# Small SBUF-to-SBUF copies on ScalarE's DMA queue while the first tiles are loaded

## The chip, the cores and the metric

One core of a Trainium2 chip runs the kernel. The metric is the device time of one execution in microseconds (us). Most of the work here is done by the core's 16 DMA engines, which move data between HBM and the on-chip SBUF; VectorE (DVE) and ScalarE (ACT) calculate, and SyncE (SP) and ScalarE issue the transfers. A transfer that is issued is cut into packets, each engine works through its share of them, and a semaphore tells when all have landed.

## The reference

Each of the 32 x 512 = 16384 rows of 1024 float32 values is divided by the sum of its absolute values:

```python
sums = np.sum(np.abs(x), axis=-1, keepdims=True)
return (x / (sums + 1e-8)).astype(np.float32)
```

The input is 67.11 MB and so is the output. Every byte goes through SBUF once.

## The kernel before

The 16384 rows are cut into 11 tiles (`rows`, line 31): ten of 12 rows per partition (128 x 12 x 1024, 6.29 MB) and a last one of 8 (4.19 MB). Four buffers of 48 KB per partition hold the tiles in turn (line 42). A tile goes through three steps.

- `load` (line 84) issues one transfer on SP's queue. `max_dma_last_dim` sets the longest piece that one packet moves: 49152 bytes for tiles 0 and 1, 24576 for the others.
- `compute` (line 97) calls `normalize` (line 45). VectorE sums the absolute values (line 47), adds the small constant (line 54), takes the reciprocal (line 56) and multiplies most rows of the tile in place (lines 58 and 65). In tiles 0 to 2 and the last two ScalarE multiplies a few rows itself (line 68); `split` on line 76 says how many.
- `store` (line 88) issues the way back on ScalarE's queue, as one transfer, or as two halves of 6 rows for the fourth and the third tile from the end (`last - 3` and `last - 2`, tiles 7 and 8). All in all there are 13 stores and 11 loads.

The order is written out by hand (lines 102 to 109): loads 0 to 3, and then for each tile its calculation, its store and the load of the tile four further on, which takes the same buffer. So load 4 waits on SP's queue until store 0 is done, load 5 until store 1, and so on; the last four stores have no load behind them.

Each DMA engine serves SP's queue (q1 in the profile) and ScalarE's queue (q10). Within a queue the packets go in the order of issue. Each of the 24 transfers ends in a packet of 4 bytes on each engine that raises its semaphore (24 x 16 = 384 packets). There are eight such semaphores for transfers, dealt out in turn; a transfer whose semaphore was used before also waits for the transfer that used it.

Of the kernel before, what the change touches and what calls it, by code (L numbers as in the profile page):

```python
# [1 line left out]

# [4 lines left out]

FP32 = mybir.dt.float32
EPS = 1e-8


@with_exitstack
def kernel(
    ctx: ExitStack,
    tc: tile.TileContext,
    x: bass.AP,
    out: bass.AP,
):
    nc = tc.nc
    P = nc.NUM_PARTITIONS  # L20

    x_flat = x.flatten_outer_dims()
    out_flat = out.flatten_outer_dims()
    n, d = x_flat.shape

    R = 12
    BUFS = 4
    HEAD = 32
    per_partition = n // P
    assert n % P == 0 and (per_partition - HEAD) % R == 0  # L30
    rows = [R] * ((per_partition - HEAD) // R + 2) + [HEAD - 2 * R]

    def piece(flat, i):
        head = flat[: P * HEAD, :].rearrange("(p r) d -> p r d", p=P)
        if i < 2:
            return head[:, R * i : R * (i + 1), :]
        if i == len(rows) - 1:
            return head[:, 2 * R :, :]
        a = P * (HEAD + R * (i - 2))
        return flat[a : a + P * R, :].rearrange("(p r) d -> p r d", p=P)  # L40

    sbuf = ctx.enter_context(tc.tile_pool(name="sbuf", bufs=BUFS))
    stats = ctx.enter_context(tc.tile_pool(name="stats", bufs=len(rows)))

    def normalize(x_tile, k, kv, kt):
        s = stats.tile([P, R], FP32)
        nc.vector.tensor_reduce(  # L47
            out=s[:, :k],
            in_=x_tile[:, :k, :],
            axis=mybir.AxisListType.X,  # L50
            op=mybir.AluOpType.add,
            apply_absolute_value=True,
        )
        nc.vector.tensor_scalar_add(out=s[:, :k], in0=s[:, :k], scalar1=EPS)  # L54
        inv = stats.tile([P, R], FP32)
        nc.vector.reciprocal(out=inv[:, :k], in_=s[:, :k])  # L56
        if kv:
            nc.vector.tensor_mul(  # L58
                out=x_tile[:, :kv, :],
                in0=x_tile[:, :kv, :],  # L60
                in1=inv[:, :kv].unsqueeze(2).to_broadcast([P, kv, d]),
            )
        for r in range(kv, kv + kt):
            row = x_tile[:, r, :]
            nc.vector.tensor_scalar_mul(out=row, in0=row, scalar1=inv[:, r : r + 1])  # L65
        for r in range(kv + kt, k):
            row = x_tile[:, r, :]
            nc.scalar.activation(  # L68
                out=row,
                in_=row,  # L70
                func=mybir.ActivationFunctionType.Copy,
                scale=inv[:, r : r + 1],
            )

    last = len(rows) - 1
    split = {0: (3, 4), 1: (0, 3), 2: (0, 3), last - 1: (0, 2), last: (5, 3)}

    tiles = {}

    HALF, WHOLE = 24576, 49152

    def load(i):
        x_tile = tiles[i] = sbuf.tile([P, R, d], FP32, name="x_tile")
        nc.sync.dma_start(out=x_tile[:, : rows[i], :], in_=piece(x_flat, i), max_dma_last_dim=WHOLE if i < 2 else HALF)  # L86

    def store(i):
        parts = [(0, R // 2), (R // 2, R)] if i in (last - 3, last - 2) else [(0, rows[i])]
        for a, b in parts:  # L90
            nc.scalar.dma_start(
                out=piece(out_flat, i)[:, a:b, :],
                in_=tiles[i][:, a:b, :],
                max_dma_last_dim=WHOLE if i >= last - 1 else HALF,
            )

    def compute(i):
        k = rows[i]
        kt, ks = split.get(i, (0, 0))
        normalize(tiles[i], k, k - kt - ks, kt)  # L100

    with tc.manual_schedule():
        for i in range(BUFS):
            load(i)
        for i in range(len(rows)):
            compute(i)
            store(i)
            if i + BUFS < len(rows):
                load(i + BUFS)


# [1 line left out]
_INS = ['x']  # L113
_OUTS = [((32, 512, 1024), 'float32')]


# [23 lines left out]
```

## Time and profile before

| what | value |
|---|---|
| median of 3 runs | 317.03 us (316.71 to 317.07) |
| profiled execution | 316.79 us, of which span 315.2 us |
| VectorE busy | 261.1 us, 51 instructions |
| ScalarE busy | 17.4 us, 16 instructions |
| VectorE waits for loads | 30.0 us in total, 17.7 of it for tile 0 |
| HBM read and written | 67.11 and 67.11 MB, 426 GB/s over the span |
| a load, issue to landing | 37.6 us (median of ten) |
| a store, issue to landing | 47.2 us (median of eight whole tiles) |

The profile is that of one execution; all instants are counted from the start of its span. Issue to landing includes the time in which a transfer stands behind others in its queue, so it is longer than the 14.5 us that 6.29 MB take at 433 GB/s. In a table by windows the columns are: the window and its length, the busy time of VectorE, ScalarE and GpSimd with their instructions, a TensorE clock (which is not used here), the share of the 16 DMA engines' time that packets took, and the GB/s of the packets that started in the window. In the list of queues the columns are packets, MB and the share of the 16 engines' time. A timeline row is start, duration, engine, line and operation; `SPq` and `ACTq` are the issues of transfers by SP and ScalarE.

### The profile page before, as it was taken

Reading aid. Unit: us, or ns where it says so; the run is one execution under the profiler, and the core shown is the slowest. Engines: PE = TensorE matmul, PEld = TensorE weight load, DVE = VectorE, ACT = ScalarE, POOL = GpSimd, SP = SyncE. Lnnn points to the kernel's source line nnn. Section 1 sums busy time; section 2 is a strip of 40 time slices with the busy share of each in tenths; the row PEclk is TensorE's granted clock in tenths of the full one; section 3 lists DMA queues with packets and bytes.
Section 4 is the critical chain, followed back from the end, with each engine's and each line's share of the span. In section 5 each row is a group of like instructions: output and inputs, shape, how many; then the busy total and the mean of one; then the engine's idle time right before and its main releaser. Section 6 shows DMA issues by size and latency. Waiting matters only on the chain.

```text
span 315.2 us, 169 instructions
## 1 busy us (share of the span) xinstructions
DVE 261.1 (83%) x51; ACT 17.4 (6%) x16; POOL 0.2 (0%) x4
## 2 busy tenths in 40 slices
DVE  0079999999999999979996997999699969999100
ACT  0010403004000000000000000000000000203000
POOL 0000000000000000000000000000000000000000
DMA  7999999999999999999999999999999999999997
GB/s 299 499 399 409 440 399 418 430 449 418 430 449 418 430 449 424 424 449 427 421 449 427 421 449 434 415 449 434 415 449 434 415 433 449 416 433 499 399 403 329
DMA packets 5504, 134.22 MB, mean 426 GB/s; under 512 B 384, under 2 KB 384, under 8 KB 384
## 3 DMA queue, kind: packets, MB, share of 16 engines
q1 hardware_dynamic: 2736, 67.11, 49.9%
q10 hardware_dynamic: 2768, 67.11, 49.4%
HBM read 67.11 MB, written 67.11 MB: 426 GB/s over the span
## 4 chain that ended last, share of the span: by engine, by line
DVE 41%; DMA 33%; another core or an unknown queue 18%; SPq 0%; issue 0%; DVEq 0%
DVE s L47 23%; DMA x_tile<-in_x_dram 17%; DVE x_tile L58 15%; DMA out_dram<-x_tile 15%; DVE x_tile L65 2%; DVE inv L56 0%; DVE s L54 0%; SPq L86 0%; DVEq L135 0%
## 5 line engine op out<-in xcount | busy, mean ns | idle before, releaser
L47 DVE TENSOR_REDUCE s<-x_tile 128x12 f32<-128x12288 f32 (+1 forms) x11 | 138.2, 12561 | 30.0 <-DMA x_tile<-in_x_dram 30.0
L58 DVE TENSOR_TENSOR x_tile<-x_tile,inv 128x12288 f32<-128x12288 f32 (+3 forms) x10 | 113.6, 11358 | 0.5
L68 ACT ACTIVATE x_tile<-x_tile,inv 128x1024 f32<-128x1024 f32 x15 | 16.1, 1138 | 257.1 <-DVE inv L56 257.1
L65 DVE TENSOR_SCALAR x_tile<-x_tile,inv 128x1024 f32<-128x1024 f32 x8 | 5.5, 748 | 0.0
L56 DVE RECIPROCAL inv<-s 128x12 f32<-128x12 f32 (+1 forms) x11 | 2.5, 226 | 0.4
L68 ACT ACT_TABLE_LOAD x1 | 1.3, 1283 | 17.8 <-DMA x_tile<-in_x_dram 17.8
L54 DVE TENSOR_SCALAR s<-s 128x12 f32<-128x12 f32 (+1 forms) x11 | 1.9, 173 | 0.4
L124 POOL MEMSET const-uint8-127<- 128x1 uint8 x1 | 0.1, 102 | 0.0
L124 POOL MEMSET const-bfloat16-1.0<- 128x1 bf16 x1 | 0.1, 101 | 0.0
L124 POOL MEMSET const-float32-0.0<- 128x1 f32 x1 | 0.1, 98 | 0.2 <-issue 0.2
L124 POOL MEMSET const-float32-1.0<- 128x1 f32 x1 | 0.1, 98 | 0.0
## 6 DMA issues: line engine op xcount, KB each, us to landing
x_tile<-in_x_dram SPq DMA_DIRECT2D x10, 6144.0 KB, 37.6
out_dram<-x_tile ACTq DMA_DIRECT2D x8, 6144.0 KB, 47.2
out_dram<-x_tile ACTq DMA_DIRECT2D x4, 3072.0 KB, 36.5
x_tile<-in_x_dram SPq DMA_DIRECT2D x1, 4096.0 KB, 32.0
out_dram<-x_tile ACTq DMA_DIRECT2D x1, 4096.0 KB, 21.7
```

Source lines behind the costliest of these rows:

```text
L47: nc.vector.tensor_reduce(out=s[:, :k], in_=x_tile[:, :k, :], axis=mybir.AxisListType.X, op=mybir.AluOpType.add, apply_absolute_value=True,)
L54: nc.vector.tensor_scalar_add(out=s[:, :k], in0=s[:, :k], scalar1=EPS)
L56: nc.vector.reciprocal(out=inv[:, :k], in_=s[:, :k])
L58: nc.vector.tensor_mul(out=x_tile[:, :kv, :], in0=x_tile[:, :kv, :], in1=inv[:, :kv].unsqueeze(2).to_broadcast([P, kv, d]),)
L65: nc.vector.tensor_scalar_mul(out=row, in0=row, scalar1=inv[:, r : r + 1])
L68: nc.scalar.activation(out=row, in_=row, func=mybir.ActivationFunctionType.Copy, scale=inv[:, r : r + 1],)
L124: nc = _bacc.Bacc("TRN2", target_bir_lowering=False, num_devices=1)
```

## The change

A second pool holds two small tiles: 128 zeros per partition, and a scratch tile of 3 x 128 values per partition that nothing reads. After load 0 has been issued, VectorE writes the zeros, and a transfer on ScalarE's queue copies them three times into the scratch tile, in pieces of 512 bytes. These are 128 x 3 = 384 packets, 24 for each of the 16 DMA engines, and one more of 4 bytes each for the semaphore. The copy stands first on ScalarE's queue, ahead of everything that ScalarE does. Loads 1 to 3 follow on SP's queue as before.

The store of tile 7 (`last - 3`) goes out as one transfer instead of two halves; its packets remain 24576 bytes long.

```diff
     sbuf = ctx.enter_context(tc.tile_pool(name="sbuf", bufs=BUFS))
+    once = ctx.enter_context(tc.tile_pool(name="once", bufs=1))
     stats = ctx.enter_context(tc.tile_pool(name="stats", bufs=len(rows)))
...
     def store(i):
-        parts = [(0, R // 2), (R // 2, R)] if i in (last - 3, last - 2) else [(0, rows[i])]
+        parts = [(0, R // 2), (R // 2, R)] if i == last - 2 else [(0, rows[i])]
...
+    CHUNKS, WIDTH = 3, 128
+
+    def fill():
+        zeros = once.tile([P, WIDTH], FP32, name="zeros")
+        nc.vector.memset(zeros, 0.0)
+        copies = once.tile([P, CHUNKS, WIDTH], FP32, name="copies")
+        nc.scalar.dma_start(
+            out=copies,
+            in_=zeros.unsqueeze(1).to_broadcast([P, CHUNKS, WIDTH]),
+            max_dma_last_dim=4 * WIDTH,
+        )
+
     with tc.manual_schedule():
-        for i in range(BUFS):
+        load(0)
+        fill()
+        for i in range(1, BUFS):
             load(i)
```

## The prediction

> **What bounds the kernel now.** I read the slices of the page first, then the DMA queues, then the same measure in short windows, because the slices hide what I needed.
>
> ```profile
> DMA  7999999999999999999999999999999999999997
> ...
> DMA packets 5504, 134.22 MB, mean 426 GB/s; under 512 B 384, under 2 KB 384, under 8 KB 384
> ...
> q1 hardware_dynamic: 2736, 67.11, 49.9%
> q10 hardware_dynamic: 2768, 67.11, 49.4%
> ```
>
> The 16 DMA engines are busy in every slice but the first and the last; the two queues (q1, SP's loads; q10, ScalarE's stores) take 99.3% of their time together. VectorE is busy for 261.1 us of 315.2 and waits 30.0 us for loads, so it is not the bound. The end is set by bytes through the DMA engines, and only two things can move it: engine time added, or engine time in which nothing flowed. Windows cut at whole packets find the second kind (the last column is GB/s):
>
> ```profile
> core 0: us, DVE busy (x) ACT busy (x) POOL busy (x), PEclk, DMA share, GB/s
> 1.70:4.30 2.60, 0.00 (x0) 0.00 (x0) 0.00 (x0) 1.00 1.09 340
> 4.30:6.11 1.81, 0.00 (x0) 0.00 (x0) 0.00 (x0) 1.00 1.00 434
> ...
> 31.90:40.07 8.17, 8.17 (x5) 3.55 (x4) 0.00 (x0) 1.00 1.00 433
> 40.07:45.52 5.45, 5.45 (x1) 0.00 (x0) 0.00 (x0) 1.00 0.99 361
> 45.52:54.60 9.08, 8.98 (x4) 2.57 (x3) 0.00 (x0) 1.00 1.01 433
> ```
>
> The rate is 433 GB/s, with loads alone (31.90 to 40.07) as with loads and stores mixed (45.52 to 54.60). It falls short in two places. The first is the start: the first 48 KB packet of each engine takes about 2.6 us where the next takes 1.81, so 0.8 us are lost before data flows. The second is 40.07 to 45.52, at 361: (433 - 361) / 433 x 5.45 = 0.9 us. (A window counts packets by their start, so it rounds; the packet records give it finer: the last two load packets ahead of the first store packet take 1131 and 1509 ns on one engine where all others of 24 KB take 912. That is 0.82 us, and the mean of the 16 engines is 0.82 too.) The second loss lies where the first store enters:
>
> ```profile
> 0.73 2.04 SPq L86 DMA_DIRECT2D x_tile<-in_x_dram  x4
> ...
> 38.75 0.42 ACTq L91 DMA_DIRECT2D out_dram<-x_tile  x1
> ```
>
> ```profile
> q1 hardware_dynamic: 63, 1.55, 99.3%
> q10 hardware_dynamic: 1, 0.02, 1.3%
> ```
>
> ```profile
> q10 hardware_dynamic: 16, 0.39, 50.4%
> q1 hardware_dynamic: 15, 0.37, 47.2%
> ```
>
> The two pairs are the queues between 38.75 and 43.19 us and between 43.19 and 45.00. The first store is issued at 38.75, its first packets start at 43.2, and from then on the queues take turns packet by packet. By the packet records neither queue runs empty again until the loads are over at 278 us, and no other loss of this size follows. So the program pays about 0.8 us once when ScalarE's queue comes to life beside a running load queue.
>
> **The change part by part.** The sum is made against the profiled execution, 316.79 us (span 315.2 and 1.6 around it). It lies 0.24 under the median of the three timed runs, 317.03; the forecast is carried to that median.
>
> *24 copies per engine: added engine time.* No row shows a 512 B packet, so I bound it. Start to start, a 49152 B packet takes 1.812 us, a 24576 B packet 0.908, a 16384 B one 0.607, a 4 B one (each transfer's completion) 6 ns. Lower bound: 24 x 6 ns = 0.14 us. Upper bound by the nearest larger row: 24 x 0.607 = 14.6 us. The four sizes lie on one line, (1.812 - 0.908) / 24576 = 36.8 ns per 1000 B and some 5 ns a packet, so 512 B take 18.8 + 5 = 24 ns. I take the line: 24 x 24 ns = **0.57 us**. It is not hidden by anything: the engines have no free time.
>
> *Do the copies break the load stream?* The 4 B packet between loads 0 and 1 (at 17.1 us) is followed by a load packet of the usual 1.815 us, so a tiny packet between large ones uncovers no latency. But it is of the same queue, so both ends stay: 0, and 24 x 0.82 = 19.7 us if every change of queue cost what the first one did. I take 0, since the mixed stretch changes queue every 0.908 us at the full 433 GB/s.
>
> *The loss at 41 us.* With the copies ScalarE's queue wakes in the first microseconds. SP's first load goes from issue at 0.73 to its first packet at 1.73, so 1.0 us. The fill waits for a memset of 128 x 128: between VectorE's 0.17 us for 12 columns and 0.75 for 1024, and VectorE is idle until 17.72. Issued at about 0.9 to 1.0, the copies arrive at about 2.0, inside the 1.73 to 2.6 in which the engines wait for first data anyway. Bounds: nothing saved (0), or all of it (-0.82 us). I take **-0.82**, because the loss lies next to the queue's waking and comes once. Whether it stays away depends on the copies still being there when the store comes. If one copy goes per load packet, 24 of them last for 16 large and 8 small load packets: 1.73 + 0.8 + 16 x 1.81 + 8 x 0.908 + 0.6 = 39.4 us, or up to 41.2 if the first copy follows the third load packet. The first tile lands 8 x 24 ns = 0.2 us later, so the store is issued at 38.95 and reaches its queue at about 40.0. That is a tie.
>
> [...] The trace's turns between 43.19 and 45.00 are of one descriptor each (16 against 15), but those are of 24 KB; no row here shows how small ones are grouped. [...]
>
> *The memset* (about 0.2 us) is hidden by VectorE's idle 17 us; uncovered it would cost those 0.2. *The fill's issue* (0.34 to 0.48 us on ScalarE) stands ahead of the table load, which waits until 17.77; behind it on that queue is only the first ACTIVATE at 31.18. SP's loads 1 to 3 are issued beside it by 2.77 and are not needed before 16 us. *The store of the fourth tile from the end in one transfer*: the same 256 packets, one completion packet per engine fewer (6 ns), which the fill's own completion gives back, and one issue of 0.4 us fewer on a ScalarE that waits 257 us. Nothing waits for that store but the end of the kernel. *Waits*: the completion semaphores are dealt in turn, so the fill shifts them: load 5 also waits for the fill, store 9 for load 8; both are over tens of microseconds before. *The tail*: the last store is issued at 292.5, and the engines run on to 313.8, so 21.3 us x 433 GB/s = 9.2 MB are queued then, 4.2 of them its own: 11 us of cover against a shift of some 0.2.
>
> Sum: +0.57 - 0.82 = -0.25 us, so 316.54 for the profiled execution and **316.8** for the median.
>
> **The rivals.**
> 1. *The loss is moved to the start* (forecast): 316.8.
> 2. *The loss stays where it is, or is paid in full at the start*, because it belongs to the first write to HBM, or because the start does not hide it. For it: the first store is also the first write to HBM, and the trace cannot part that from the queue's waking. Against it: nothing but that the loss precedes the store's first packet. 317.03 + 0.57 = 317.6, from 317.2 to 318.2 if a copy costs 6 ns or twice the line.
> 3. *Slower than before: the queue runs dry.* The copies end before the store's descriptors arrive, and an empty queue wakes at a price each time: one loss in the first load, one at 41 us. It decides if the copies end before about 40 us and the start hides nothing. 317.03 + 0.57 + 0.82 = 318.4.
> 4. *Every copy uncovers the latency of the next load packet*: 317.03 + 19.7 = 336.7 at worst. The 4 B row speaks against it.
> 5. *The copies are nearly free*, by the lower bound: -0.82 + 0.14, so 316.35, down to 316.2 at no cost. For it: only the 4 B row.
>
> **How the numbers follow.** Forecast 0.45, rival 2 0.30, rival 3 0.13, rival 4 0.02, rival 5 0.10. A measurement of this kernel can tell about 0.2%, 0.63 us, from no change: 316.4 to 317.66. Faster by more: rival 5, and 0.06 of the forecast's own spread, 0.16. Within: 0.39 of the forecast and 0.20 of rival 2, 0.59. Slower: 0.10 of rival 2 (dear copies), rivals 3 and 4, 0.25. The range runs from rival 5's 316.2 to rival 2's 318.2 and leaves out rivals 3 and 4, 0.15. The likeliest case alone gives 316.4 to 317.3 (copies of 6 to 47 ns).
>
> **What would show it.** Right: in the changed profile's windows of whole packets 433 GB/s through 40 to 45 us; 5888 packets, of which 768 are under 2 KB; copies of about 24 ns spread over the first 39 us; the first 48 KB packets no longer than 2.6 us. [...] The prediction fails if the loss is tied to the first HBM write, or if a small packet costs much over the line.

## The result and the profile after

The changed kernel takes 317.56 us (median of 11 runs, 317.48 to 317.93), the kernel before 316.84 in 11 runs beside it. The medians are 0.72 us apart; the ratio of the means is 1.0026, with a 95% interval of 1.0018 to 1.0034, so the change is slower. The forecast was 0.25 us faster. The profiled execution takes 317.50 us with a span of 315.7, against 316.79 and 315.2.

The slices and the queues of the changed kernel:

```profile
DMA  7999999999999999999999999999999999999997
...
DMA packets 5888, 134.42 MB, mean 426 GB/s; under 512 B 384, under 2 KB 768, under 8 KB 768
...
q1 hardware_dynamic: 2736, 67.11, 49.7%
q10 hardware_dynamic: 3152, 67.31, 49.5%
```

384 packets came to ScalarE's queue, and the engines are as full as before (99.2% of their time, before 99.3%). The windows tell more (the last column is GB/s):

```profile
core 0: us, DVE busy (x) ACT busy (x) POOL busy (x), PEclk, DMA share, GB/s
6.05:17.07 11.02, 0.00 (x0) 0.00 (x0) 0.00 (x0) 1.00 1.00 433
...
40.26:45.71 5.45, 5.45 (x1) 0.00 (x0) 0.00 (x0) 1.00 1.01 388
45.71:54.79 9.08, 8.98 (x4) 2.42 (x3) 0.00 (x0) 1.00 1.00 430
```

In the first row loads and copies run in turn at the full 433 GB/s: the copies break nothing. In the second row the loss is back, in the very place where the kernel before has it: (433 - 388) / 433 x 5.45 = 0.57 us, by the packet records 0.61 on the mean of the engines, where the kernel before has 0.82 by the same count. (One trace of each is too little to call the difference a gain: e6 below has the same copies and loses 0.97.) The fill's own rows:

```profile
0.83 0.17 DVE L107 MEMSET zeros<- 128x128 f32 x1 [0.83 <-PEq L139]
1.02 0.66 ACTq L109 DMA_DIRECT2D copies<-zeros  x1
```

```profile
copies<-zeros ACTq DMA_DIRECT2D x1, 192.0 KB, 39.3
```

It is issued at 1.02 and lands 39.3 us later, at 40.3. By the packet records its first copies start at 6.06 to 6.63 us, behind the second load packet of each engine; from there on nearly always one copy goes per load packet, mostly 23 or 24 ns from start to start. An engine's last copy starts at 38.4 to 39.0 us. The first store is issued at 39.09 and its first packets start at 43.6 to 44.8, so ScalarE's queue has nothing to send in some 4 us ahead of them.

The last place that differs is behind the last transfer, in what SP waits for at the end (total, times, longest), before and after:

```profile
SPq L135 <- PEq L135: 0.6, 2, 0.4
```

```profile
SPq L150 <- PEq L150: 0.9, 2, 0.8
```

When all data have landed the engines meet twice at a barrier. One of the two meetings takes 0.8 us instead of 0.4; by the trace the late comer is VectorE. Its last DRAIN (by its semaphores in the trace, the instruction with which an engine reports to that meeting) is finished 0.95 us after the last store's wait instead of 0.42. The rows of ScalarE and VectorE, before and after (ns shortest/median/longest, first and last start in us):

```profile
L135 ACTq DRAIN  x2: 8/80/153, 292.9 to 314.6; - x2
L135 DVEq DRAIN  x2: 19/1725/3431, 289.0 to 314.6; - x2
L135 ACTq EVENT_SEMAPHORE  x2: 17/17/17, 314.5 to 314.9; - x2
L135 DVEq EVENT_SEMAPHORE  x2: 21/21/21, 314.5 to 315.1; - x2
```

```profile
L150 ACTq DRAIN  x2: 8/80/153, 293.4 to 314.9; - x2
L150 DVEq DRAIN  x2: 125/1779/3433, 289.6 to 315.4; - x2
```

The 0.71 us between the two profiled executions are then: 0.35 until the last engine's last packet (313.85 to 314.20), 0.21 more between that store's wait and the end of the span, and 0.15 more outside the span (1.63 to 1.79).

### The profile page after: what moved, and what is told of

Same layout as the page of the kernel before. It is cut to its first block, busy times and chain, and to the rows that moved or that the text cites. A ratio compares the mean times of both kernels' runs of the same rounds, so it can differ in the third digit from the quotient of the medians.

```text
span 315.7 us, 171 instructions
## 1 busy us (share of the span) xinstructions
DVE 261.4 (83%) x52; ACT 17.4 (6%) x16; POOL 0.2 (0%) x4
## 4 chain that ended last, share of the span: by engine, by line
DVE 41%; DMA 33%; another core or an unknown queue 18%; SPq 0%; issue 0%; DVEq 0%
DVE s L48 23%; DMA x_tile<-in_x_dram 17%; DMA out_dram<-x_tile 15%; DVE x_tile L59 15%; DVE x_tile L66 1%; DVE inv L57 0%; DVE s L55 0%; SPq L87 0%; DVEq L150 0%
## 6 DMA issues: line engine op xcount, KB each, us to landing
copies<-zeros ACTq DMA_DIRECT2D x1, 192.0 KB, 39.3
```

## The experiments

Each kernel is the kernel before or the changed one with the edit shown (and the pool `once` added where the kernel before needs a small tile). "Loss at 41" is what the load packets around the first store of a tile take beyond their usual time, as a mean of 16 engines. Differences in us are between medians, intervals are those of the ratio.

**One part alone, and more copies**

```diff
# e1_merge_only: the kernel before, with
-        parts = ... if i in (last - 3, last - 2) else [(0, rows[i])]
+        parts = ... if i == last - 2 else [(0, rows[i])]
# e2_four_chunks: the changed kernel, with
-    CHUNKS, WIDTH = 3, 128
+    CHUNKS, WIDTH = 4, 128
```

> The kernel before with only the store of tile 7 in one transfer; no copies. All theories: no change, within 0.1 us of the kernel before, and the loss of 0.8 us where the first store enters stays. If this part carried some of the measured +0.72 us, the time would be above the kernel before by over 0.2 us.

Measured 316.89 us against 316.84, ratio 1.0002 (0.9993 to 1.0011). The store in one transfer carries nothing that can be told from noise.

> The changed kernel with 32 copies per engine instead of 24, so that by one copy per load packet they last until 46 to 47 us and the queue is never empty when the first store reaches it (about 40 us). Theory A (a queue that wakes from empty costs the engines about 0.7 us each time): the loss at 41 to 44 us is gone, 8 x 24 ns = 0.19 us are added, so about 0.5 us under the changed kernel and 0.2 us above the kernel before. Theory B (the loss belongs to the first store itself: first write to HBM, or first large packet read from SBUF): the loss moves to where the first store packet now stands, at about 47 us, and the time is 0.19 us above the changed kernel, 0.9 above the kernel before.

Measured 317.86 us, 1.02 above the kernel before (ratio 1.0031, 1.0020 to 1.0043) and 0.30 above the changed kernel. An engine's last copies now start between 44.8 and 46.6 us, and the copies' completion packet goes right ahead of the first store packet, at 47.4 to 48.1 us, so ScalarE's queue never runs dry. The loss comes all the same, on the load packets ahead of the store's new place (0.86 by the packet records):

```profile
44.00:49.45 5.45, 5.45 (x1) 0.00 (x0) 0.00 (x0) 1.00 1.01 365
49.45:58.53 9.08, 8.98 (x4) 3.23 (x3) 0.00 (x0) 1.00 1.00 433
```

Theory A, an empty queue that wakes at a price, falls.

**One small packet in the middle of the loads**

```diff
# e3_wake_copy: the kernel before, with, between the first loads and compute(0),
+        scratch = once.tile([P, 128], FP32, name="scratch")
+        nc.scalar.dma_start(out=scratch[:16, :], in_=tiles[0][:16, 0, :128])
# e4_wake_hbm: the same place
+        nc.scalar.dma_start(out=piece(out_flat, last)[:16, 0, :128], in_=tiles[0][:16, 0, :128])
```

> The kernel before with one single 512-byte copy per engine, SBUF to SBUF, on ScalarE's queue as soon as tile 0 has landed (17.7 us), in the middle of the loads. Theory A: load packets at 19 to 22 us are longer by about 0.7 us, the loss at 41 to 43 us comes again, time +0.7 us over the kernel before. Theory B: no loss at 20 us, the usual one at 41 us, time within 0.1 us of the kernel before. A third possibility (a queue costs this once, at its first use): loss at 20 us and none at 41, time unchanged.

> As the single copy, but the 512 bytes per engine go from tile 0 to HBM, into the output rows of the last tile, which its own store overwrites at the end. Theory A: a loss of 0.7 us at 20 us and one at 41 us, time +0.7 us. Theory B in the form of the first write to HBM: loss at 20 us, none at 41, time unchanged. Theory B in the form of the first large packet from SBUF: none at 20 us, the usual one at 41, time within 0.1 us.

In both traces the load packets at 19 to 25 us keep their 1815 ns, though ScalarE's empty queue wakes there, in e4 with a write to HBM. The loss at 41 comes as usual (0.79 and 0.76 us). For e3, two stretches around the copy and the place of the loss:

```profile
20.40:22.21 1.81, 1.81 (x1) 0.00 (x0) 0.00 (x0) 1.00 1.00 433
22.21:24.05 1.84, 1.84 (x1) 0.00 (x0) 0.00 (x0) 1.00 1.00 432
40.07:45.52 5.45, 5.45 (x1) 0.00 (x0) 0.00 (x0) 1.00 0.99 365
```

So it is neither a queue's waking nor its first use, nor the first write to HBM, at least not one of 512 bytes. The times are 317.28 and 317.13 us, 0.44 and 0.29 above the kernel before (1.0005 to 1.0023, 1.0004 to 1.0021), which no theory had asked for: the packets end where they did (mean 313.48 and 313.44 us, before 313.54). What both share with the changed kernel is that VectorE runs 65 instructions in the trace (waits and drains counted) instead of 64, here through one more wait, and that the span goes on 0.2 us longer after the last store.

**The one VectorE instruction**

```diff
# e5_memset_only: the kernel before, with, after load(0),
+        zeros = once.tile([P, 128], FP32, name="zeros")
+        nc.vector.memset(zeros, 0.0)
# e6_memset_gpsimd: the changed kernel, with
-        nc.vector.memset(zeros, 0.0)
+        nc.gpsimd.memset(zeros, 0.0)
# e8_fewer_dve: the kernel before, with one row of the last tile moved to ScalarE
-    split = {..., last: (5, 3)}
+    split = {..., last: (4, 4)}
```

> The kernel before with the memset of 128 x 128 zeros on VectorE at the start and no copies at all. Theory C (one VectorE instruction more, 65 in the trace instead of 64, delays VectorE's last instructions behind the last transfer): +0.3 to +0.4 us over the kernel before, none of it in the transfers: the last packets end when they did, and the span goes on 0.2 us longer after them. Rival (the memset is hidden by VectorE's idle start, and the extra time of the changed kernel is in the transfers alone): no change.

Measured 317.21 us against 316.88: +0.33, ratio 1.0009 (1.0000 to 1.0018), so by the time alone it is at the edge of the noise. The packets end no later (last 313.79, before 313.85), and the barrier's long meeting is there, without a single copy:

```profile
SPq L139 <- PEq L139: 0.9, 2, 0.8
```

> The changed kernel with its memset on GpSimd instead of VectorE; the copies stay. Theory C: 0.3 to 0.4 us under the changed kernel, so 317.2 where the kernel before has 316.84, with 64 VectorE instructions in the trace. Rival: as the changed kernel, 317.5 to 317.6.

Measured 317.29 us: 0.27 under the changed kernel, 0.41 above the kernel before (1.0002 to 1.0020). 64 VectorE instructions, and the short meeting again, with all the copies; the loss at 41 is 0.97, against 0.82 in the kernel before:

```profile
SPq L150 <- PEq L150: 0.6, 2, 0.4
```

```profile
40.26:45.71 5.45, 5.45 (x1) 0.00 (x0) 0.00 (x0) 1.00 1.00 356
```

> The kernel before with one row of the last tile moved from VectorE to ScalarE, so that VectorE has 63 instructions in the trace instead of 64; the last store is issued about 1.2 us later, which its 11 us of cover hide. Theory C in the form that each VectorE instruction over a limit delays one more instruction at the end: 0.1 to 0.3 us under the kernel before. Theory C as a step between 64 and 65 alone: no change. Rival: no change.

Measured 317.04 us against 316.88, ratio 1.0005 (0.9996 to 1.0014): no gain from 63. So it is not a price for each instruction. The traces say more: wherever there is a 64th VectorE instruction, it is the one that comes late. In the five kernels with 64 it is the last one, the wait at the second meeting (before: 315.13 us, the others 314.95 at the latest), behind which nobody waits. In the nine with 65 it is the DRAIN of that meeting, some 0.4 us behind the others', and all engines wait for it: from the last packet to the end of the span they take 1.51 to 1.57 us instead of 1.30 to 1.35, and 1.77 to 1.80 us lie outside the span instead of 1.63 to 1.65 (means over the runs). In e8, with 63, that tail is shorter, 1.16 us, but 1.98 us lie outside the span, which takes the gain away.

**Larger packets in the middle of the loads**

```diff
# e7_big_store_early: 24576 bytes per engine, to HBM
+        nc.scalar.dma_start(out=piece(out_flat, last)[:16, :6, :],
+            in_=tiles[0][:16, :6, :], max_dma_last_dim=HALF)
# e9_copy_8k_early: 8192 bytes per engine, to SBUF (scratch of 2 rows)
+        nc.scalar.dma_start(out=scratch[:16, :, :], in_=tiles[0][:16, :2, :], max_dma_last_dim=8192)
# e10_store_8k_early: 8192 bytes per engine, to HBM
+        nc.scalar.dma_start(out=piece(out_flat, last)[:16, :2, :],
+            in_=tiles[0][:16, :2, :], max_dma_last_dim=8192)
# e11_hbm_8k_start: 8192 bytes per engine, HBM to HBM, right after load(0)
+        nc.scalar.dma_start(out=piece(out_flat, last)[:16, :2, :],
+            in_=piece(x_flat, last)[:16, :2, :], max_dma_last_dim=8192)
```

> The kernel before with one store packet of 24576 bytes per engine, from tile 0 to output rows that the last store overwrites, as soon as tile 0 has landed. It adds 0.91 us of engine time and, by theory C, 0.35 us at the end. Theory D (the loss is paid whenever a large store packet enters a stream of loads alone): load packets near 20 to 22 us longer by 0.7 to 0.8 us, the loss at 41 to 43 us again, time +2.0 us over the kernel before. Theory E (paid once, by the first large store packet of the program): loss at 20 us and none at 41, time +1.3 us. Theory F (paid by the lasting change from loads alone to loads and stores in turn, not by one packet): none at 20 us, the usual one at 41, time +1.3 us.

Measured 319.13 us, +2.25 (1.0062 to 1.0088). The early packet itself takes 1.37 us too long on the mean, and then the loss at 41 is gone (0.01):

```profile
22.30:24.70 2.40, 2.40 (x1) 0.00 (x0) 0.00 (x0) 1.00 1.08 225
...
40.07:45.52 5.45, 5.45 (x1) 0.00 (x0) 0.00 (x0) 1.00 1.00 433
```

So here the loss is paid once. The time is above theory E's +1.3: the payment was larger than 0.8, and the engines' ends lie further apart; it probably left the engines out of step (their last packets end from 314.14 to 315.54, before from 313.33 to 313.85).

> The kernel before with one SBUF-to-SBUF copy of 8192 bytes per engine at about 20 us (tile 0 to a scratch tile). It adds 0.31 us of engine time and 0.35 us for one VectorE instruction more. Theory G (the one-time loss belongs to the first large packet that is read from SBUF): a loss of up to 0.8 us at 20 to 25 us and none at 41 to 43, time +0.66 us over the kernel before. Theory H (it belongs to the first large write to HBM): no loss at 20 us, the usual one at 41, time +0.66 us too: the trace decides, not the time.

> As the 8 KB copy, but to HBM (output rows of the last tile, overwritten at the end). Theories G and H: loss of 0.8 us or less at 20 to 25 us, and none, or only the rest of 0.8 us, at 41 to 43. If 8192 bytes are too few for it: none at 20 us, the usual one at 41. Time +0.66 us over the kernel before in either case.

317.73 and 317.72 us, +0.87 and +0.86 (1.0017 to 1.0040, 1.0017 to 1.0038): the same time, two traces. The copy held the engines up at 22 to 25 us, and the loss at 41 is gone (0.03); the store held nobody up, and the loss is there (1.0). So a first store packet of 8 KB in a loads-only stream does not bring the loss by itself. The copy first, then the store, each at its packet and at 40 us:

```profile
22.10:25.10 3.00, 3.00 (x1) 0.00 (x0) 0.00 (x0) 1.00 0.99 306
...
40.07:45.52 5.45, 5.45 (x1) 0.00 (x0) 0.00 (x0) 1.00 1.01 433
```

```profile
22.10:24.22 2.12, 2.12 (x1) 0.00 (x0) 0.00 (x0) 1.00 1.00 433
...
40.07:45.52 5.45, 5.45 (x1) 0.00 (x0) 0.00 (x0) 1.00 0.96 334
```

> The kernel before with one HBM-to-HBM copy of 8192 bytes per engine (from the input to output rows of the last tile, overwritten at the end) on ScalarE's queue right at the start, in the shadow of the wait for the first data. Adds 0.31 us of engine time and no VectorE instruction. Theory H with a loss that the start hides: no loss at 41 us, time 0.3 to 0.5 us under the kernel before. Theory H with a loss that is only moved: a long packet in the first 6 us, none at 41, +0.3 us. Theory G: the usual loss at 41 us, +0.3 us.

317.29 us, +0.43 (1.0005 to 1.0023): no hold-up between the first packets and 39 us, the usual loss at 41 (0.76). It was meant to fall into the wait for the first data and did not: its packets start at 5.9 to 6.6 us, behind the second load packet, as the copies of the changed kernel do. Whether a loss that early would be hidden was therefore not tried by any run.

**A hold-up without a store and without ScalarE's queue**

```diff
# e12_load_4ports: the kernel before, with, on SP's queue between load(0) and load(1),
+        nc.sync.dma_start(out=scratch[:16, :, :], in_=piece(x_flat, last)[:16, :2, :], max_dma_last_dim=8192)
# e13_copy_8k_all: the 8 KB copy at 20 us, over 128 partitions, 8 packets of 8192 bytes per engine
+        nc.scalar.dma_start(out=scratch[:, :, :], in_=tiles[0][:, :2, :], max_dma_last_dim=8192)
```

> The kernel before with one more load of 8192 bytes per engine on SP's own queue, between loads 0 and 1, into 16 neighbouring partitions of a scratch tile. Nothing is read from SBUF and ScalarE's queue is not touched. In the 8 KB copy to 16 neighbouring partitions the engines were held up for about 1 us, and the loss at 41 us did not come. Theory J (any hold-up of about that length, whatever its cause, is the same one-time payment: the stream then runs with more in flight): the engines are held up for 0.8 to 1.2 us at 17 to 21 us and there is no loss at 41; time +0.3 us for the bytes, +0.2 to 0.4 for the longer hold-up. Theory G (it takes a large packet read from SBUF): the usual loss at 41, whatever happens at 17; if there is a hold-up, time +1.3 us.

317.41 us, +0.56 (1.0006 to 1.0025). The engines are held up by 0.85 us at 17 us, and at 41 there is next to nothing left (0.04):

```profile
16.96:19.86 2.90, 1.20 (x1) 1.15 (x1) 0.00 (x0) 1.00 1.03 316
...
40.03:45.48 5.45, 5.45 (x1) 0.00 (x0) 0.00 (x0) 1.00 0.99 424
```

This transfer reads nothing from SBUF, writes nothing to HBM and stands on SP's queue. Theory G falls, and what theory J expected to see is seen. The bytes alone would take an engine 0.31 us, by the line through the larger packets; the 0.85 come on top. What makes the transfer so slow is not shown: no run here made the same load into other partitions.

> [...] Adds 8 x 0.306 = 2.45 us of engine time and one VectorE instruction (0.35 us). Theory G: a loss of 0.8 us at 20 to 30 us, none at 41; +2.8 us. Theory J: no hold-up at 20 to 30 us and the usual loss at 41; +2.8 us too. The trace decides.

319.38 us, +2.53 (1.0067 to 1.0096). No single hold-up of 0.8 us: 0.40 at 31 to 33 us and smaller ones from 17 us on, 0.62 in all, and none at 41 (0.01). Theory J had expected no hold-up and the usual loss (that 128 partitions would hold nobody up was an estimate that no run had shown), so here it missed, and theory G's line (a loss before 34 us, none at 41) comes closer. With G ruled out by e12, the reading that fits both runs is that small hold-ups count towards the same payment; that is argued from this one run.

## Why the prediction was wrong, point by point

*What bounds the kernel*: right. The DMA engines stay full (99.2% of their time), and the only things that moved the end through them were bytes and hold-ups. The rest of the change came behind the last transfer.

*The copies, 24 x 24 ns = 0.57 us*: right in size. Start to start they mostly take 23 to 24 ns in the trace, and with the memset off VectorE the copies cost +0.41 us (0.06 to 0.63 by the interval of e6). The load packets beside them keep their 1.81 us, so rival 4 is out; the small 24 KB load packets between the last copies take mostly 915 to 921 ns instead of 912, 0.05 us in all.

*One copy per turn*: right. The turns of the profile before were of 24 KB packets (16 against 15) and left open how small ones go; the trace has one 512 B packet per turn in 372 of 378 turns, until 38.4 to 39.0 us.

*The loss at 41 us, -0.82*: wrong, and the step that failed is the reason given for it, "because the loss lies next to the queue's waking and comes once". "Comes once" is right, the waking is not the cause: the queue wakes at 20 us without a loss (e3, e4), and the loss comes at a queue that has not been empty (e2). Neighbourhood in time was taken for cause; the first store brings several first things at once, and the prediction named one rival among them, the first write to HBM, which e4 rules out for 512 bytes and e10 for 8 KB. What the runs show in its place: the loads-only stream loses some 0.6 to 1.4 us once. If nothing held the engines up before, the loss stands at the first 24 KB store packets (0.61 to 1.00 in eleven kernels; the two with the 24 copies have 0.61 and 0.97). If something did, by 0.62 to 1.37 us in all (e7, e9, e12, e13), 0.04 at most is left there. A transfer that holds up nobody leaves it where it is (e3, e4, e10, e11). This is a rule read off these runs, not a mechanism. Theory J's reason for it, a stream that afterwards runs with more in flight, has no row in any trace and was not shown; why the loss comes at the first stores is open too.

*When the copies come and go*: two terms of the same step were mis-sized. The prediction let a transfer's first packet follow its issue by 1.0 us, as SP's first load does on idle engines. With loads ahead it takes 4.4 to 5.2 us in the traces: the fill goes from 1.02 to 6.06, the first store from 38.75 to 43.2 before and from 39.09 to 43.6 after. So the copies did not come "inside the 1.73 to 2.6", and what was called a tie at about 40 us was none: the last copy starts at 39.0 at the latest, over 4 us ahead of the first store packet. The condition "the copies still being there when the store comes" was not met, but e2 meets it and has the loss, so this is not what the forecast failed by.

*The memset, 0.17 us, hidden by VectorE's idle start*: the second step that failed. Its 0.17 us are hidden. Its being there is not: with 65 VectorE instructions VectorE is late at the barrier behind the last transfer, +0.33 us (e5), and e6 takes 0.27 of it back. The profile before could have raised the doubt, since VectorE is there already the last at the final barrier, by 0.18 us; the size could not be read from it.

*The sum*: +0.33 (e5) and +0.41 (e6) make 0.74, and 0.72 was measured; with intervals of 0.00 to 0.57 and 0.06 to 0.63 behind the two, so close a match is partly luck. In the prediction's terms that is rival 2 (+0.57, the loss stays) with the memset's price on top, which would be 0.90. The merged store (e1) carries nothing that shows; the shifted waits were not tried alone.

No run points to a kernel that beats the one before. In these runs the loss was moved and not avoided: each transfer that took it away at 41 us paid 0.62 us or more earlier, with its own bytes besides.

## What to carry to other kernels

A dip in the transfer rate beside an event is not yet the price of that event: list all that happens there for the first time, and let a run do each of these things alone before counting the dip as a gain. In this kernel, whose DMA engines never rest, a 512 B copy took 23 to 24 ns, some 5 more than its bytes by the line through the larger packets, while one more instruction on VectorE, which is idle 17% of the time, cost as much as some 14 of them (0.33 us in e5 against 0.024), where it delayed that engine at the last barrier; so compare the rows behind the last transfer too.

## What was not expected of the hardware

- One VectorE instruction more, 65 instead of 64 in the trace, cost +0.33 us with no other change; 63 brought nothing. In all 14 traces that have a 64th VectorE instruction it is the late one. What delays it wasn't tried.
- A loss of about 0.8 us per engine that a loads-only stream shows once: 0.82 at the first store, or 0.85 at a load into 16 partitions at 17 us (then 0.04 at the first store).
- With loads ahead on SP's queue, 4.4 to 5.2 us pass from an issue on ScalarE's queue to its first packet; on idle engines SP's first load takes 1.0 us.
- 8 KB per engine into 16 neighbouring partitions held the engines up by 0.85 us (load) and 1.0 us (copy); 8 KB out of 16 neighbouring partitions to HBM held up nobody, 24 KB out of them did by 1.37 us.
